# Layer 1's FFN down projection turned over: tokens on the partitions, scaled there, transposed back and added to x

## The chip, the core and the metric

The kernel runs on one core of a Trainium2 chip. The metric is the device time of one execution in microseconds. Engines are named as in the profile: PE is TensorE's matrix multiplication and PEld its weight loads, DVE is VectorE, ACT is ScalarE, POOL is GpSimd, SP is SyncE, which here only issues DMAs.

## The reference, cut to what matters

Two layers of a streaming encoder over 256 tokens of width 2048. Each layer ends with a gated convolutional FFN whose output is normalised and added to x. The change touches the last step of layer 1:

```python
def rms_norm(x, g):
    y = x * lax.rsqrt(jnp.mean(x * x, axis=-1, keepdims=True) + NORM_EPS)
    return y * g

def channel_mixer(h, up, conv_w, conv_b, down):      # h (256, 2048), up (2048, 8192), down (4096, 2048)
    hid = causal_dwconv(h @ up, conv_w, conv_b)
    gate, val = jnp.split(hid, 2, axis=-1)
    return (jax.nn.gelu(gate, approximate=True) * val) @ down

f = channel_mixer(h, ffn_up[layer], ffn_conv_w[layer], ffn_conv_b[layer], ffn_down[layer])
x = x + rms_norm(f, ffn_post_g[layer])               # for layer 1 this is the output
```

## The kernel before

**Layout.** x lies in SBUF as xT, 128 partitions by 16 feature tiles by 256 tokens: features are on the partitions, tokens in the free dimension. The output leaves in the same order, so that the runs of a DMA that writes all tokens of n feature tiles are n KB long on each partition.

**Precision by three products.** Every float32 weight piece is split into a high part wh and a rest wl, both float32r. An activation tile x has a high and a low half too. A product is wh·x.hi + wl·x.hi + wh·x.lo. In the form called WIDE the two halves of x lie side by side and form one moving operand of 512 columns: for each weight tile of 128 x 128 one matmul of 512 columns with wh as the weights (L225) and one of 256 columns with wl (L228). In the narrow form there are three matmuls of 256 columns (function three, L208 to L210). Function tok_chunk, which layer 0 uses for its value projection, does it the other way round: the activation tile is loaded as the weights, and 512 columns of wh or wl are streamed (L300 to L302), with one accumulator bank for each of the two tiles of 128 tokens.

**Pieces.** Weights come in pieces of 2 tiles of 128 rows by 512 columns (512 KB), issued on SP's queue into 4 raw buffers. ACT makes wh (L155), DVE makes wl (L156), each with 5 buffers. Function take hands the next piece to the caller and, before it does so, emits the splits up to 4 pieces ahead and the DMAs behind them. The order of the pieces is a list written out in advance (plan). Function between runs jobs that fell due after a piece; in layer 1's down projection no job is queued. Within an engine the order is the program's, except that an instruction that is ready earlier can be placed ahead of one that is not.

**Layer 1's down projection, norm and last sum.** out_proj makes four chunks of 512 output features, each over 32 tiles of the hidden width, that is 16 pieces. In the first three chunks the form is WIDE, one bank for each tile of 128 features; when a chunk is complete, ACT copies one half of each bank, DVE adds the other (merge), ACT squares the result, DVE sums the squares, and ACT multiplies by the gain (gained). In the fourth chunk two of its four tiles take the narrow form, so that they need no merge. A product with a matrix of ones adds the squares up over the partitions and gives every partition the sum for each token (L749, L757). Then finish takes the root (root, L353 to L359) and goes through the 16 feature tiles in the hand-written order TAIL: DVE and POOL take turns with one or two tiles, multiply by the root (L463), add x (L464) and write out, DVE's parts on SP's queue and POOL's on ACT's (L465).

**SBUF tiles.** The normalised input xg of this FFN lies in the hpool tiles H6, H10, H7 and H8 and is read for the last time by the last up projection chunk. The projected output mg lies in H6 and H10.

Of the kernel before, what the change touches and what calls it, by code (L numbers as in the profile page):

```python
# [9 lines left out]
F32 = mybir.dt.float32  # L10
F32R = mybir.dt.float32r
I32 = mybir.dt.int32
AF = mybir.ActivationFunctionType
# [3 lines left out]
P = 128  # L17
T = 256
D = 2048
# [14 lines left out]
ROOT = 15  # L34
EARLY = 6
SINGLE = 2

TAIL = (("v", 1), ("p", 1), ("v", 2), ("p", 1), ("v", 2), ("p", 1), ("v", 2), ("p", 1), ("v", 2), ("p", 1), ("v", 2))
LRU_EARLY = 4
BEF = 3  # L40


# [17 lines left out]
def trunk(ctx: ExitStack, tc: tile.TileContext, a: dict, out: bass.AP):  # L60
# [10 lines left out]
    def nm(s):  # L71
        cnt[0] += 1
        return f"{s}_{cnt[0]}"
# [4 lines left out]
    def w2(shape):  # L78
        return spool.tile(shape, F32, tag="w2", name=nm("w2"), bufs=7)

    def acc_bank(shape):
        return psum.tile(shape, F32, tag="ps", name=nm("acc"))

    def ms_bank(shape):
        return psum.tile(shape, F32, tag="ps", name=nm("ms"))
# [73 lines left out]
    def behind_pieces(fn):  # L159

        with tc.issue_after(state["act"].ins), tc.issue_after(state["dve"].ins):
            return fn()
# [8 lines left out]
    def take(tag):  # L171
        i = state["take"]
        state["take"] += 1
        ahead(i + PIECES - 1)
        j = jobs[i]
        assert j["tag"] == tag, (j["tag"], tag)
        return j["hi"], j["lo"], j["k0"], j["n"]
# [4 lines left out]
    def later(pieces, fn):  # L182
        state["seq"] += 1
        queue.append((state["count"] + pieces, state["seq"], fn))
# [126 lines left out]
    def big(idx, dt=F32):  # L311
        return [H(i, dt) for i in idx]
# [21 lines left out]
    def at(b):  # L334
        def f(k, n=None):
            t = b[k // 8]
            return t[:, k % 8, :] if n is None else t[:, k % 8:k % 8 + n, :]
        return f
# [6 lines left out]
    def bc(r, n=2):  # L345
        return r[:, None, :].to_broadcast([P, n, T])


    def root(ps, n, tag, with_table=None, with_step=None):

        r = spool.tile([P, T], F32, tag=f"r_{tag}", name=nm("rstd"))
        t = w1()
        i = nc.scalar.activation(r, ps, AF.Abs_reciprocal_sqrt, bias=eps_c[:, 0:1], scale=1.0 / n)  # L353
        early = with_table(r, i) if with_table else None
        nc.vector.scalar_tensor_tensor(t, r, -0.5 / n, r, op0=ALU.mult, op1=ALU.mult)
        nc.vector.scalar_tensor_tensor(t, ps, n * EPS, t, op0=ALU.add, op1=ALU.mult)
        if with_step:
            with_step(t, early)
        nc.vector.scalar_tensor_tensor(r, t, 1.5, r, op0=ALU.add, op1=ALU.mult)  # L359
        return r  # L360
# [90 lines left out]
            else:  # L451
                later(k - EARLY + 1, lambda k=k: step(k, 2))

    def finish(mg, st):
        st["rest"]()
        rs = root(st["ps"], D, "post")
        ft = big((7, 8))
        k = 0
        for e, n in TAIL:
            eng = nc.vector if e == "v" else nc.gpsimd  # L460
            xs = xT[:, k:k + n, :]
            t = ft[k // 8][:, k % 8:k % 8 + n, :]
            eng.tensor_tensor(t, mg(k, n), bc(rs, n), op=ALU.mult)  # L463
            eng.tensor_tensor(xs, xs, t, op=ALU.add)  # L464
            (nc.sync if e == "v" else nc.scalar).dma_start(out[:, k:k + n, :], xs)  # L465
            k += n


    S0, S1 = slice(0, P), slice(P, P + T)
# [298 lines left out]
    def ffn(layer, mg, st, xgi, hi_, mgi):  # L768
# [42 lines left out]
        load_table(last[-1])  # L811
        if layer == 0:
            later(4, lambda: behind_pieces(tables))
        mg2 = at(big(mgi))
        st2 = out_proj(f"d{layer}", layer, hid, 32, "ffn_post_g", mg2, ("mix_pre_g", 1) if layer == 0 else None)
        return mg2, st2
# [268 lines left out]
    mg = at(big((4, 5)))  # L1085
    st = out_proj("cdo", 1, oc + od, 16, "mix_post_g", mg, ("ffn_pre_g", 1), CD_ORDER)
    flush()
    mg, st = ffn(1, mg, st, (6, 10, 7, 8), (9, 11, 0, 1, 2, 3, 4, 5), (6, 10))
    finish(mg, st)


# [48 lines left out]
```

## Time and profile before

| what | value |
|---|---|
| time, median of 3 runs | 1745.57 us (1744.69 to 1745.91) |
| the profiled execution's own time | 1744.74 us |
| its span, from the first to the last instruction | 1743.0 us |
| PE busy | 1721.8 us (99% of the span) |
| PEld busy | 1551.9 us (89%) |
| DVE busy | 1221.3 us (70%) |
| ACT busy | 983.6 us (56%) |
| POOL busy | 37.8 us (2%) |
| DMA traffic | 314.92 MB, 181 GB/s in the mean |

Busy times of PE overlap each other, since matmuls are pipelined: the distance between the starts of two matmuls is what each costs, not its own duration. The chain that ended last is the sequence of instructions that, followed back from the end, each set the start of the next. The granted clock is given as a share of 2.4 GHz.

### The profile page before, as it was taken

The page shows a single profiled execution, that of the slowest core. Times are in us where ns is not written, and L with a number is a line of the kernel's source. Part 1 is how long each engine was busy: PE and PEld are TensorE (multiplying, and loading weights), DVE is VectorE, ACT ScalarE, POOL GpSimd, SP SyncE. Part 2 cuts the span into 40 slices and gives each one's busy share as a digit, 9 for nine tenths or more (in the row PEclk, how much of TensorE's full clock was granted, in tenths as well). Part 3 has the DMA queues.
Part 4 walks back from the last instruction along what each step waited for, and adds up shares of the span by engine and source line. Part 5 has one row for each costly group of instructions (what it writes and reads, how often), then busy time and mean ns, then how long its engine had stood idle before and what let it go on. Part 6 is the DMA issues. An engine that isn't in the chain of part 4 may idle for free.

```text
span 1743.0 us, 27768 instructions
## 1 busy us (share of the span) xinstructions
PE 1721.8 (99%) x10786; PEld 1551.9 (89%) x10786; DVE 1221.3 (70%) x1839; ACT 983.6 (56%) x1511; POOL 37.8 (2%) x117
## 2 busy tenths in 40 slices
PE   9999999999999999999999999999999999999995
PEld 9888888999888888888999999899988888888895
DVE  7675667588777777855468996658877777774544
ACT  6445554566555555654446875656655555554441
POOL 0000000000000000000000010000000000000002
PEclk9999999999999999999999999999999999999998
DMA  8566555655666666565556545555566666656552
GB/s 275 175 208 188 157 154 170 184 161 179 198 189 192 186 190 192 185 195 189 185 159 180 158 146 166 173 183 162 176 205 186 189 193 186 190 192 187 189 182 72
DMA packets 165027, 314.92 MB, mean 181 GB/s; under 512 B 12064, under 2 KB 15264, under 8 KB 164896
## 3 DMA queue, kind: packets, MB, share of 16 engines
q1 hardware_dynamic: 163184, 310.13, 58.0%
q0 software_dynamic: 560, 2.10, 0.4%
q8 instruction: 84, 1.38, 0.3%
q10 hardware_dynamic: 1152, 0.93, 0.2%
q14 instruction: 47, 0.39, 0.1%
HBM read 311.02 MB, written 2.10 MB: 180 GB/s over the span
## 4 chain that ended last, share of the span: by engine, by line
PE 96%; DVE 3%; ACT 1%; issue 0%; DMA 0%; DVEq 0%; ACTq 0%
PE acc L225 47%; PE acc L228 24%; PE acc L208 5%; PE acc L210 5%; PE acc L209 5%; PE ms L209 2%; PE ms L208 2%; PE ms L210 2%; PE acc L300 1%; PE acc L302 1%; PE acc L301 1%; DVE wl L156 1%; PE ms L717 0%; PE ms L497 0%; PE ms L905 0%
## 5 line engine op out<-in xcount | busy, mean ns | idle before, releaser
L156 DVE TENSOR_TENSOR wl<-wr,wh 128x1024 fp32r<-128x1024 f32 (+2 forms) x592 | 714.7, 1211 | 459.3 <-ACT wh L155 457.7
L155 ACT CAST wh<-wr 128x1024 fp32r<-128x1024 f32 (+2 forms) x592 | 611.9, 1037 | 598.4 <-PE acc L225 360.4
L225 PE MATMUL acc<-H,wh 128*128 128x512 f32 x3520 | 912.9, 394 | 0.0
L225 PEld LDWEIGHTS acc<-H,wh 128*128 128x128 f32 x3520 | 621.7, 189 | 100.0
L228 PEld LDWEIGHTS acc<-H,wl 128*128 128x128 f32 x3520 | 502.3, 190 | 49.4
L228 PE MATMUL acc<-H,wl 128*128 128x256 f32 x3520 | 515.4, 282 | 0.0
L208 PE MATMUL acc<-H,wh 128*128 128x256 f32 (+1 forms) x736 | 210.8, 287 | 0.8 <-ACT H L391 0.8
L209 PE MATMUL acc<-H,wl 128*128 128x256 f32 (+1 forms) x736 | 207.7, 282 | 0.0
L210 PE MATMUL acc<-H,wh 128*128 128x256 f32 (+1 forms) x736 | 207.5, 283 | 0.0
L208 PEld LDWEIGHTS acc<-H,wh 128*128 128x128 f32 (+1 forms) x736 | 139.1, 189 | 1.8 <-ACT H L391 1.4
L209 PEld LDWEIGHTS acc<-H,wl 128*128 128x128 f32 (+1 forms) x736 | 139.1, 189 | 0.3
L210 PEld LDWEIGHTS acc<-H,wh 128*128 128x128 f32 (+1 forms) x736 | 139.0, 189 | 0.0
L283 ACT COPY w<-acc 128x256 f32<-128x256 f32 x192 | 70.3, 370 | 64.2 <-PE acc L228 64.2
L208 PE MATMUL ms<-H,wh 128*128 128x256 f32 x256 | 73.0, 285 | 0.0
L209 PE MATMUL ms<-H,wl 128*128 128x256 f32 x256 | 72.3, 283 | 0.0
L210 PE MATMUL ms<-H,wh 128*128 128x256 f32 x256 | 72.3, 283 | 0.0
L787 ACT ACTIVATE w<-w,pk 128x256 f32<-128x256 f32 x128 | 69.4, 593 | 1.7 <-DVE w L781 1.2
L788 DVE SCALAR_TENSOR_TENSOR w<-w,pk,w 128x256 f32<-128x256 f32 x128 | 56.7, 481 | 1.3 <-ACT w L787 1.1
L789 DVE SCALAR_TENSOR_TENSOR w<-w,pk,w 128x256 f32<-128x256 f32 x128 | 56.2, 480 | 0.0
L284 DVE TENSOR_TENSOR w<-acc,w 128x256 f32<-128x256 f32 x120 | 49.8, 420 | 2.8 <-ACT w L283 1.1
L208 PEld LDWEIGHTS ms<-H,wh 128*128 128x128 f32 x256 | 49.1, 192 | 0.1
L209 PEld LDWEIGHTS ms<-H,wl 128*128 128x128 f32 x256 | 49.1, 192 | 0.1
(225 smaller groups left out, 1101.7 us busy)
## 6 DMA issues: line engine op xcount, KB each, us to landing
wr<-in_ffn_up SPq DMA_DIRECT2D x256, 512.0 KB, 4.5
wr<-in_ffn_down SPq DMA_DIRECT2D x128, 512.0 KB, 3.9
wr<-in_ab_w_in SPq DMA_DIRECT2D x78, 512.0 KB, 3.6
wr<-in_cd_w_in SPq DMA_DIRECT2D x40, 512.0 KB, 4.4
wr<-in_ab_w_out SPq DMA_DIRECT2D x32, 512.0 KB, 4.4
wr<-in_cd_w_out SPq DMA_DIRECT2D x32, 512.0 KB, 4.2
wr<-in_w_q_up SPq DMA_DIRECT2D x8, 384.0 KB, 3.9
wr<-in_cd_w_in SPq DMA_DIRECT2D x8, 320.0 KB, 3.0
```

What stands on the lines that cost most here:

```text
L155: state["act"] = nc.scalar.copy(hi, j["raw"])
L156: state["dve"] = nc.vector.tensor_tensor(lo, j["raw"], hi.bitcast(F32), op=ALU.subtract)
L208: nc.tensor.matmul(ps, wh, x.hi(k), start=start, stop=False, skip_group_check=True)
L209: nc.tensor.matmul(ps, wl, x.hi(k), start=False, stop=False, skip_group_check=True)
L210: return nc.tensor.matmul(ps, wh, x.lo(k), start=False, stop=stop, skip_group_check=True)
L225: mm = nc.tensor.matmul(banks[b], hi[:, kk, c], x.both(korder[i] if korder else i), start=i == 0, stop=False, skip_group_check=True)
L228: mm = nc.tensor.matmul(banks[b][:, 0, :], lo[:, kk, c], x.hi(korder[i] if korder else i), start=False, stop=i == ks - 1, skip_group_check ...
L283: nc.scalar.copy(t, bank[:, 1, :])
L284: nc.vector.tensor_tensor(dst, bank[:, 0, :], t, op=ALU.add)
L787: nc.scalar.activation(t[:, j, :], u[:, j, 2:], AF.Identity, scale=cw[2], bias=col("ffn_conv_b", layer, i))
L788: nc.vector.scalar_tensor_tensor(t[:, j, :], u[:, j, 1:1 + T], cw[1], t[:, j, :], op0=ALU.mult, op1=ALU.add)
L789: nc.vector.scalar_tensor_tensor(t[:, j, :], u[:, j, 0:T], cw[0], t[:, j, :], op0=ALU.mult, op1=ALU.add)
```

## The change

Layer 1's last projection no longer goes through out_proj and finish. Function last_sum, called at the end of ffn for layer 1, does this instead:

- A row of the 2048 gains is gathered by a DMA on POOL's queue from pk (where they lie 128 to a column) to partition 0 of gb, which is H7. Seven more DMAs on the same queue double it: 1 partition to 2, to 4, up to 128. Each needs the one before.
- Chunks 0 to 2 go through tok_chunk. After each, for both token tiles, take_out lets ACT square the bank with the sum along the row collected in ss, and DVE multiply the bank by the gains into u (H6 for token tile 0, H10 for tile 1). Sums are thus scalars per partition, so that no product with ones is needed. The sums of three chunks are added up and prepared for the root (pre_b, pre_n).
- Chunk 3 goes on for 14 pieces with both token tiles in turn. The last two pieces (AHEAD = 4 tiles of the hidden width) are taken together: all 12 matmuls of token tile 0 come first, then 9 of token tile 1, and its last 3 stand in the program behind the first 8 transposes of token tile 0.
- The root of a token tile is one ACT instruction and three DVE instructions of one column (last_root). Four parts of 512 features are scaled by it, on DVE and ACT in turn (scaled). Function back turns a part over with four transposes on PE into one bank, DVE adds the bank to xT, and SP's queue writes out 4 feature tiles by 128 tokens, 256 KB in runs of 512 bytes.
- The table TAIL and function finish are gone, and POOL has no arithmetic left at the end.

```diff
--- before.py
+++ after.py
@@ -34,9 +34,9 @@
 ROOT = 15
 EARLY = 6
 SINGLE = 2
-
-TAIL = (("v", 1), ("p", 1), ("v", 2), ("p", 1), ("v", 2), ("p", 1), ("v", 2), ("p", 1), ("v", 2), ("p", 1), ("v", 2))
 LRU_EARLY = 4
+
+AHEAD = 4
 BEF = 3
 
 
@@ -451,19 +451,103 @@
             else:
                 later(k - EARLY + 1, lambda k=k: step(k, 2))
 
-    def finish(mg, st):
-        st["rest"]()
-        rs = root(st["ps"], D, "post")
-        ft = big((7, 8))
-        k = 0
-        for e, n in TAIL:
-            eng = nc.vector if e == "v" else nc.gpsimd
-            xs = xT[:, k:k + n, :]
-            t = ft[k // 8][:, k % 8:k % 8 + n, :]
-            eng.tensor_tensor(t, mg(k, n), bc(rs, n), op=ALU.mult)
-            eng.tensor_tensor(xs, xs, t, op=ALU.add)
-            (nc.sync if e == "v" else nc.scalar).dma_start(out[:, k:k + n, :], xs)
-            k += n
+    def last_sum(pref, layer, o, ks, gname, u, gb):
+
+
+        u = [t.rearrange("p k t -> p (k t)") for t in u]
+        gb = gb.rearrange("p k t -> p (k t)")
+
+        c0 = _COL[gname][0] + 16 * layer
+        with nc.allow_non_contiguous_dma(reason="a row of gains"):
+            nc.gpsimd.dma_start(gb[0:1, :], a["pk"][:, c0:c0 + KD].rearrange("p k -> k p"))
+        n = 1
+        while n < P:
+            nc.gpsimd.dma_start(gb[n:2 * n, :], gb[0:n, :])
+            n *= 2
+        ss = spool.tile([P, 2, 4], F32, tag="sm", name="ss", bufs=4)
+        pre_b = spool.tile([P, 2], F32, tag="rcol", name=nm("pre"), bufs=2)
+        pre_n = spool.tile([P, 2], F32, tag="rcol", name=nm("pre"), bufs=2)
+        rs = spool.tile([P, 2], F32, tag="rcs", name="rs")
+        tn = spool.tile([P, 2], F32, tag="lz", name="tn")
+
+        def part(c):
+            return slice(512 * c, 512 * c + 512)
+
+        def take_out(c, b, bank):
+            nc.scalar.activation(w2([P, 512]), bank, AF.Square, accum_out=ss[:, b, c:c + 1])
+            nc.vector.tensor_tensor(u[b][:, part(c)], bank, gb[:, part(c)], op=ALU.mult)
+
+        for c in range(3):
+            for b, bank in enumerate(tok_chunk(f"{pref}{c}", o, ks, 512)):
+                take_out(c, b, bank)
+        for b in range(2):
+            nc.vector.tensor_tensor(tn[:, b:b + 1], ss[:, b, 0:1], ss[:, b, 1:2], op=ALU.add)
+            nc.vector.tensor_tensor(tn[:, b:b + 1], tn[:, b:b + 1], ss[:, b, 2:3], op=ALU.add)
+        nc.vector.tensor_scalar(pre_b, tn, 1.0 / D, EPS, op0=ALU.mult, op1=ALU.add)
+        nc.vector.tensor_scalar(pre_n, tn, D * EPS, None, op0=ALU.add)
+
+        banks = [acc_bank([P, 512]) for _ in range(2)]
+
+        def products(b, tiles):
+            for hi, lo, kk, k in tiles:
+                xh, xl = o.hi(k)[:, b * P:(b + 1) * P], o.lo(k)[:, b * P:(b + 1) * P]
+                nc.tensor.matmul(banks[b], xh, hi[:, kk, :], start=k == 0, stop=False)
+                nc.tensor.matmul(banks[b], xh, lo[:, kk, :], start=False, stop=False)
+                mm = nc.tensor.matmul(banks[b], xl, hi[:, kk, :], start=False, stop=k == ks - 1)
+            return mm
+
+        def last_root(b):
+            r, t, s = rs[:, b:b + 1], tn[:, b:b + 1], ss[:, b, 3:4]
+            nc.scalar.activation(r, s, AF.Abs_reciprocal_sqrt, bias=pre_b[:, b:b + 1], scale=1.0 / D)
+            nc.vector.scalar_tensor_tensor(t, r, -0.5 / D, r, op0=ALU.mult, op1=ALU.mult)
+            nc.vector.scalar_tensor_tensor(t, s, pre_n[:, b:b + 1], t, op0=ALU.add, op1=ALU.mult)
+            nc.vector.scalar_tensor_tensor(r, t, 1.5, r, op0=ALU.add, op1=ALU.mult)
+
+        def scaled(b, c):
+            v = u[b][:, part(c)]
+            if c % 2:
+                nc.scalar.activation(v, v, AF.Copy, scale=rs[:, b:b + 1])
+            else:
+                nc.vector.tensor_scalar(v, v, rs[:, b:b + 1], None, op0=ALU.mult)
+
+        def back(b, c):
+            pt = ms_bank([P, 4, P])
+            for j in range(4):
+                nc.tensor.transpose(pt[:, j, :], u[b][:, 512 * c + P * j:512 * c + P * j + P], ident)
+            xs = xT[:, 4 * c:4 * c + 4, b * P:(b + 1) * P]
+            nc.vector.tensor_tensor(xs, xs, pt, op=ALU.add)
+            nc.sync.dma_start(out[:, 4 * c:4 * c + 4, b * P:(b + 1) * P], xs)
+
+        done = 0
+        while done < ks - AHEAD:
+            hi, lo, k0, n = take(f"{pref}3")
+            for kk in range(n):
+                for b in range(2):
+                    mm = products(b, [(hi, lo, kk, k0 + kk)])
+            done += n
+            between(mm)
+        tiles = []
+        while done < ks:
+            hi, lo, k0, n = take(f"{pref}3")
+            tiles += [(hi, lo, kk, k0 + kk) for kk in range(n)]
+            done += n
+        products(0, tiles)
+        take_out(3, 0, banks[0])
+        last_root(0)
+        products(1, tiles[:-1])
+        for c in range(4):
+            scaled(0, c)
+        back(0, 0)
+        back(0, 1)
+        products(1, tiles[-1:])
+        take_out(3, 1, banks[1])
+        back(0, 2)
+        back(0, 3)
+        last_root(1)
+        for c in range(4):
+            scaled(1, c)
+        for c in range(4):
+            back(1, c)
 
 
     S0, S1 = slice(0, P), slice(P, P + T)
@@ -811,6 +895,8 @@
         load_table(last[-1])
         if layer == 0:
             later(4, lambda: behind_pieces(tables))
+        if layer == 1:
+            return last_sum("d1", 1, hid, 32, "ffn_post_g", big(mgi), H(7))
         mg2 = at(big(mgi))
         st2 = out_proj(f"d{layer}", layer, hid, 32, "ffn_post_g", mg2, ("mix_pre_g", 1) if layer == 0 else None)
         return mg2, st2
@@ -1085,8 +1171,7 @@
     mg = at(big((4, 5)))
     st = out_proj("cdo", 1, oc + od, 16, "mix_post_g", mg, ("ffn_pre_g", 1), CD_ORDER)
     flush()
-    mg, st = ffn(1, mg, st, (6, 10, 7, 8), (9, 11, 0, 1, 2, 3, 4, 5), (6, 10))
-    finish(mg, st)
+    ffn(1, mg, st, (6, 10, 7, 8), (9, 11, 0, 1, 2, 3, 4, 5), (6, 10))
 
 
 # ---- launch: one core ----
```

## Rows read from the trace of the kernel before

**Rows 1.** Busy time by stage, whole windows: window, length, engines, clock, DMA, GB/s
```profile
1541.60:1675.60 134.00, 134.00 (x770) 117.83 (x769) 72.70 (x83) 64.38 (x87) 0.00 (x0) 1.00 0.60 189
1675.60:1724.40 48.80, 48.80 (x341) 45.60 (x341) 20.66 (x25) 19.33 (x31) 0.00 (x0) 1.00 0.34 108
1724.40:1743.00 18.60, 1.13 (x5) 0.33 (x3) 13.33 (x15) 1.91 (x5) 10.69 (x10) 0.59 0.32 113
```

**Rows 2.** Chain that ended last, in the tail: start, length, engine and line
```profile
1724.28 0.14 PE acc L210
...
1727.81 1.55 DVE H L463 x2
```

**Rows 3.** Timeline of PE, chunks 0 and 3 of the down projection: start, busy time
```profile
1541.61 0.63 PE L225 MATMUL acc<-H,wh 128*128 128x512 f32 x2
...
1675.67 0.63 PE L225 MATMUL acc<-H,wh 128*128 128x512 f32 x2
...
1703.96 1.09 PE L225 MATMUL acc<-H,wh 128*128 128x512 f32 x4
```

**Rows 4.** Timeline of PE in layer 0's value projection, the token form
```profile
57.29 0.40 PE L300 MATMUL acc<-wh,H 128*128 128x512 f32 x1
...
59.82 0.39 PE L302 MATMUL acc<-wh,H 128*128 128x512 f32 x1
...
89.19 0.39 PE L301 MATMUL acc<-wl,H 128*128 128x512 f32 x1
...
108.23 0.39 PE L301 MATMUL acc<-wl,H 128*128 128x512 f32 x1
```

**Rows 5.** DMA issues by line: KB each, us from issue to landing
```profile
out_x<-xT SPq DMA_DIRECT2D x5, 256.0 KB, 2.1
...
H<-in_lru_wa POOLq DMA_DIRECT2D x1, 512.0 KB, 6.2
...
pk<-in_pk ACTq DMA_DIRECT2D x1, 8.0 KB, 3.0
```

**Rows 6.** Groups of instructions by line, shapes apart: busy us, mean ns
```profile
L883 POOL DMA_DIRECT2D H<-in_lru_wa x1 | 0.9, 899 | 189.1 <-PE acc L210 189.1
L481 ACT ACTIVATION_READ_ACCUMULATOR w<-w,sm 128x1 f32 x32 | 6.0, 187 | 0.0
L399 ACT ACTIVATE w<-acc 128x256 f32<-128x256 f32 x8 | 3.1, 384 | 6.4 <-PE acc L210 6.4
L659 ACT ACTIVATE H<-acc,rcol 128x512 f32<-128x512 f32 x4 | 2.8, 690 | 2.3 <-PE acc L302 2.3
L783 DVE TENSOR_TENSOR w<-ms,rstd 128x512 f32<-128x512 f32 x4 | 2.7, 684 | 0.0
L103 ACT ACTIVATE eps_c<-eps_c 128x1 f32<-128x1 f32 x6 | 1.2, 203 | 0.1
L637 DVE TENSOR_SCALAR score<-w,wT 128x256 f32<-128x256 f32 x1 | 0.3, 344 | 0.0
L637 DVE TENSOR_SCALAR score<-w,wT 128x128 f32<-128x128 f32 x1 | 0.3, 280 | 0.0
L839 DVE TENSOR_SCALAR lz<-pk 128x8 f32<-128x8 f32 x1 | 0.2, 163 | 0.0
```

**Rows 7.** Timeline of PE, three transposes of 128 x 128 in a row
```profile
176.57 0.49 PE L490 MATMUL ms<-ident,w 128*128 128x128 f32 x3
```

**Rows 8.** Timeline of DVE in the tail, its last adds
```profile
1731.28 2.34 DVE L463 TENSOR_TENSOR H<-H,rstd 128x512 f32<-128x512 f32 x2
...
1738.06 1.80 DVE L464 TENSOR_TENSOR xT<-xT,H 128x512 f32<-128x512 f32 x2
```

**Rows 9.** DMA queues from 1725 us on: packets, MB, share of 16 engines' 18.1 us
```profile
q1 hardware_dynamic: 864, 1.44, 21.5%
q10 hardware_dynamic: 720, 0.66, 10.9%
```

**Rows 10.** Busy time by window in the tail, with the granted clock
```profile
1728.00:1730.00 2.00, 0.00 (x0) 0.00 (x0) 2.00 (x3) 0.00 (x0) 2.00 (x3) 0.50 0.00 0
```

## The prediction

> **What bounds the kernel now.** I read the busy time by stage first, cut at the start of layer 1's down projection and at its last matmul. From 1541.6 to 1724.4 us PE is busy all the time at the full granted clock, DVE and ACT about half of it, and the DMA engines a third to 60% [rows 1]. So 182.8 us go at PE's pace, and a change there counts only if it alters the number or the spacing of matmuls. The last 18.6 us are another stage: PE has 1.1 us of work, DVE 13.3, POOL 10.7. The chain of waits, read next, shows it in order: a last matmul from 1724.28 to 1724.42, then square and root, and from 1727.81 on DVE's multiplications and adds only [rows 2]. DVE's adds of 128x512 take far longer there than its usual 0.684 us: the four multiplications and adds in a row from 1731.28 to 1735.88 need about 1.15 each, with POOL at work on the same kind beside it [rows 6, 8]. The last add ends at 1738.06 + 1.80 = 1739.86; the span ends at 1743.0, so 3.14 us are the write-out and what closes the program [rows 8, 1]. Two stages, two separate terms.
>
> **The matmuls' spacing.** Before, piece 1 of chunk 0 starts at 1541.61 and piece 1 of chunk 3 at 1675.67, with 48 pieces between: 2.793 us a piece [rows 3]. In chunk 3, with two tiles in the narrow form, ten pieces take 1703.96 - 1675.67 = 28.29, 2.829 each [rows 3]. A piece in token form is 12 matmuls of 512 columns: as many columns as before (3072 per tile of the hidden width), in 12 instructions where there were 16 or 20. What one costs there is in layer 0's value projection: undisturbed, 84 matmuls from 89.19 to 108.23, 0.2267 each; at its start, behind another form, 11 from 57.29 to 59.82, 0.230 each [rows 4]. So a piece costs 2.72 (at worst 2.76). There the activation is the loaded operand too, and the loads of it are hidden behind 512 columns, so I carry it over; I take the undisturbed value, because no queued job breaks into these chunks. By 62 pieces (all but the last two) the time before would be 48 x 2.793 + 14 x 2.829 = 173.7; after, 62 x 2.72 = 168.7 (at worst 171.1). **Term one: -5.0 us** (bounds -2.6 and, if the trace's spacing does not carry over, 0). The last two pieces then start at t0 = 1541.61 + 168.7 = 1710.3.
>
> **Work beside PE.** Squares and multiplications at the chunk ends (two of each, 0.7 to 0.8 us each) are fewer than the copies, merges, squares, sums and gains that they replace; DVE and ACT have more than 40% spare [rows 1] and up to four split pieces lie ready, so they cost nothing. Without that cover, a delay of DVE would stop PE after four pieces, 10.9 us.
>
> **The row of gains.** It can start when H7 is free, at 1541.6, and is needed at the first take_out, 16 x 2.72 = 43.5 us later. No row shows such a gather. Nearest are three: pk's 8 KB in 3.0 us, lru_wa on POOL's queue in 6.2 us for 1024 runs of 512 bytes, and 2.1 for an output of 256 KB [rows 5]; POOL spends 0.9 on issuing one [rows 6]. Gather: from 0.9 + 3.0 to 0.9 + 2 x 6.2 (2048 runs), 3.9 to 13.3. Each doubling: 0.9 + 2.1 to 0.9 + 6.2, 3.0 to 7.1, seven times. Sum 25 to 63 us. Six doublings are small, nearest to pk's 3.9, the last carries 512 KB, 7.1; with the gather at its upper end this is 13.3 + 6 x 3.9 + 7.1 = 44 us. That is level with 43.5. But DVE waits behind prepared pieces: a multiplication that is stuck holds up the splits of L156 queued behind it, and PE feels this only when the four pieces are used up, less one split, some 8 us later. The limit is 51.5 us, so I put this at nothing; the upper end would stall PE by 63 - 51.5 = 11.5 us.
>
> The Trainium skill's page "DMA: Bandwidth & Descriptors" (section Rules for kernel authors) speaks against this gather: a last dim that isn't contiguous becomes one descriptor per element, so 2048 of 4 bytes. By its section Anatomy of one DMA (about 2.0 us fixed for each DMA from GpSimd, the bytes at 436 GB/s) the eight DMAs, about 1 MB, would need an estimated 18.4 us beside what the descriptors cost. The sum would be the same by either. No run here shows the gather.
>
> **The tail, from t0.** Token tile 0's 12 matmuls start at 0; the last one begins at 11 x 0.2267 = 2.5 and ends 0.39 later, at 2.9. ACT's square of 512 from PSUM: 0.384 for 256 [rows 6], about 0.6 for 512, plus 0.187 to read the sum, to 3.75; the root on one column 0.2 [rows 6], to 4.0. DVE's three small steps at 0.163 [rows 6] end at 4.6. Scaling on DVE: 0.280 for 128 columns and 0.344 for 256 [rows 6] give 0.47 for 512 by the same slope; on ACT 0.69 [rows 6]. PE is through with token tile 1's 9 matmuls at 21 x 0.2267 = 4.75 and can turn over the first part at 5.2, three transposes in a row take 0.49 [rows 7], so four at most 0.65. Whether PE's last three matmuls come before or after the first transposes, they end by 6.9.
>
> From 5.85 on DVE decides. Adds from PSUM take 0.684 [rows 6]: two adds to 7.2, the multiplication of token tile 1 to 7.9, two adds to 9.25, the root to 9.75 (its square has long been done on ACT), two scalings to 10.7, a first add at 10.95, the fourth done at 13.7. Some 0.03 us between DVE instructions, 14 of them, make it **14.2**. Before, it was 1739.86 - (1541.61 + 173.7) = 24.5 behind the same place in the pieces.
>
> Behind it, the write-out. It was 3.14 us with runs of 1 and 2 KB. From the queues: 864 packets of 1.67 KB on average took 0.215 x 16 x 18.1 = 62 us of engine time, 72 ns each; 720 of 0.92 KB took 44 ns [rows 9]. That line gives some 29 ns at 0.5 KB; 512 such runs over 16 engines are 0.93 us for 256 KB, against 0.7 between adds. Three times 0.2 late: 0.6 us. Bounds: 0 if transfers are absorbed, 1.5 if a 0.5 KB run costs 44 ns like the larger ones. End: 1710.3 + 14.2 + 3.14 + 0.6 = **1728.2**, against 1743.0: **-14.8 us** in all, so -9.8 for the tail. One cost I leave at zero: PE waits some 3 us for token tile 1's scaling, and in the old tail, in a window in which PE had nothing, the clock stood at 0.50 [rows 10]; four transposes at half clock are 0.9, which would add 0.2 to each of four adds, 0.8 us.
>
> The profiled execution took 1744.74, 0.83 below the median of 1745.57; taken off the median, this is **1730.8 us**.
>
> **Rivals.**
> 1. *PE's spacing does not improve.* The ready DMA and split work could hold it at 2.79, since the fast stretch is only 19 us of another layer. Against it: that stretch ran beside the same splits. Term one falls away: 1735.8. Chance 0.1.
> 2. *The gains come late.* By the rows the chain is 25 to 63 us with 51.5 allowed; for it speaks that my middle (44) is near. PE stalls by up to 11.5 us: 1731 to 1742, about 1737. Chance 0.1.
> 3. *Slower: the gather runs on one DMA engine.* It ends in a single partition, and its 2048 elements might all go through one queue. lru_wa's 1024 runs on 16 engines are 64 each in 6.2 us, 97 ns a run; 2048 in one queue would be 199 us, and with doublings of 30.5 the stall is 199 + 30.5 - 51.5 = 178 us: about 1909. It decides from a gather of 51.5 + 14.8 - 30.5 = 35.8 us upward, 17.5 ns an element: that eats the whole gain. Against it: a load of 8 KB took 3.0 us, though in other runs [rows 5]. Chance 0.06. Beside this stands the page's rule "Use all 16 engines" (same section): the engines are chosen by the access patterns' slowest dim, here 16 tiles at the source; by that the gather is spread.
>
> **How the numbers follow.** The forecast has 0.74. Its own range is 1728 (write-out free, DVE at 13.7) to 1735 (spacing 0.230: +2.4; runs of 0.5 KB: +0.9; half clock: +0.8). The whole range goes to 1738, which takes in rival 1 and half of rival 2, and to 1727.5 below. A difference under 0.2%, 3.5 us, can't be told from none here: all of the forecast and rival 1 and most of rival 2 lie below 1742. Faster 0.91, same 0.02, slower 0.07.
>
> **What would show it.** L300-like matmuls in layer 1 at 0.227 spacing, and a first matmul of the last two pieces near 1710; POOL's eight DMAs over before 1585, DVE's first gain multiplication not waiting for a DMA; the last matmul of a product near 1717; DVE without gaps of more than 0.3 us from its first scaling to its last add near 1724.5, with adds near 0.69 since POOL is silent; the last landing some 3 to 4 us later. I am wrong if PE idles in chunk 1, if PE's pieces take 2.79, or if the write-out queues up by microseconds.

## The result, and the profile after

The changed kernel takes **1734.03 us** (median of 6 runs, 1733.01 to 1734.96); the kernel before, on the same chip, 1745.74 (6 runs, 1744.69 to 1746.76). The ratio is 0.9933 [0.9924, 0.9943], a difference of 11.7 us. The profiled execution of after took 1733.38 with a span of 1731.6, against 1744.74 and 1743.0: its spans differ by 11.4 us, and that is the sum to be explained.

The page's line of busy times, of the changed kernel:

```profile
PE 1719.7 (99%) x10492; PEld 1538.4 (89%) x10492; DVE 1210.5 (70%) x1829; ACT 976.2 (56%) x1486; POOL 31.8 (2%) x115
```

PE is busy for all but 11.9 us of the span. To see where, the windows of layer 1's down projection, cut by the new code (columns as in [rows 1]):

```profile
1545.00:1713.70 168.70, 168.70 (x747) 139.68 (x746) 84.78 (x90) 72.03 (x83) 3.72 (x8) 1.00 0.61 186
1713.70:1720.40 6.70, 6.65 (x35) 5.34 (x34) 2.63 (x8) 2.32 (x5) 0.00 (x0) 1.00 0.00 0
1720.40:1731.60 11.20, 3.29 (x25) 2.65 (x23) 6.28 (x14) 2.32 (x5) 0.00 (x0) 0.72 0.66 187
```

These are the pieces up to the last two, then the matmuls of these two, then the tail. The first answers to the two first windows of [rows 1]: PE without a gap at full clock. The last answers to their third: 11.2 us where there were 18.6, with POOL silent.

Where does the projection begin? The timeline of PE, changed kernel:

```profile
1542.22 0.63 PE L225 MATMUL acc<-H,wh 128*128 128x512 f32 x2
...
1544.77 0.40 PE L228 MATMUL acc<-H,wl 128*128 128x256 f32 x2
1545.01 0.40 PE L300 MATMUL acc<-wh,H 128*128 128x512 f32 x1
...
1713.67 0.39 PE L494 MATMUL acc<-wh,H 128*128 128x512 f32 x1
```

The first new matmul (L300) is at 1545.01. In the 2.79 us ahead of it stands a piece of the old form, in which L225 and L228 take turns in twos. [rows 3] have the same pattern at 1541.61, and the prediction took it for the projection's first piece. It is the *last piece of the chunk before* (a chunk's last piece does its products bank by bank). So the projection of the kernel before starts at 1541.61 + 2.79 = 1544.40, which the timeline of that kernel shows too. Its last two pieces start at 1718.13:

```profile
1544.40 1.09 PE L225 MATMUL acc<-H,wh 128*128 128x512 f32 x4
...
1718.13 1.09 PE L225 MATMUL acc<-H,wh 128*128 128x512 f32 x4
```

From here on **S** is the first matmul of layer 1's down projection: 1544.40 before, 1545.01 after. S differs from profile to profile (1544.4 to 1546.4 in the runs below), and between before and after the difference is there from the start: PE's first matmul of L270 begins at 5.54 before and at 6.13 in after. Executions of one kernel differ as much (spans of 1731.2 to 1733.2 for after). So profiles are compared by their distance from S.

The chain of waits at the end, changed kernel:

```profile
1716.59 0.70 ACT w L477 x2
1717.31 0.69 DVE H L478
...
1718.56 0.50 DVE H L511
1719.10 0.67 PE ms L516 x4
1719.79 1.88 DVE xT L518 x3
1721.67 0.60 DVE H L478
1722.28 0.59 DVE xT L518
...
1723.43 0.50 DVE H L511
1723.97 0.67 PE ms L516 x4
1724.66 1.88 DVE xT L518 x3
1726.55 0.60 DVEq L1221
```

It reads as the prediction's tail did: square (L477), gain (L478), scaling (L511), transposes (L516), adds (L518), once for each token tile, with tile 1's gain between tile 0's adds. What is new is that the gain follows the square of the same bank instead of running beside it. PE's wait for tile 1's scaling, put at some 3 us, is 2.67 (up to 1723.97). The timeline gives the same with the idle times:

```profile
1717.31 0.69 DVE L478 TENSOR_TENSOR H<-acc,H 128x512 f32<-128x512 f32 x1 [9.29 <-ACT w L477]
...
1720.46 0.60 ACT L477 ACTIVATE w<-acc 128x512 f32<-128x512 f32 x1 [0.57 <-PE acc L496]
...
1723.97 2.39 PE L516 MATMUL ms<-ident,H 128*128 128x128 f32 x16 [2.67 <-DVE H L511]
1724.66 2.48 DVE L518 TENSOR_TENSOR xT<-xT,ms 128x512 f32<-128x512 f32 x4 [0.35 <-PE ms L516]
```

The last add ends at 1724.66 + 2.48 = 1727.14, and 4.46 us later the span ends. The three terms, then, with t0 as the first matmul of the last two pieces:

| | before | after | change | forecast |
|---|---|---|---|---|
| S to t0 | 173.73 | 168.66 | -5.1 | -5.0 |
| t0 to the last add's end | 21.73 | 13.47 | -8.3 | -10.4 |
| last add's end to the span's end | 3.14 | 4.46 | +1.3 | +0.6 |
| S itself | 1544.40 | 1545.01 | +0.6 | 0 |
| span | 1743.0 | 1731.6 | **-11.4** | -14.8 |

(t0 is 1718.13 before and 1713.67 after, by the rows above.)

### The profile page after: what moved, and what is told of

It is laid out like the page before. It is cut to its first block, busy times and chain, and to the rows that moved or that the text cites. A ratio compares the mean times of both kernels' runs of the same rounds, so it can differ in the third digit from the quotient of the medians.

```text
span 1731.6 us, 27137 instructions
## 1 busy us (share of the span) xinstructions
PE 1719.7 (99%) x10492; PEld 1538.4 (89%) x10492; DVE 1210.5 (70%) x1829; ACT 976.2 (56%) x1486; POOL 31.8 (2%) x115
## 4 chain that ended last, share of the span: by engine, by line
PE 96%; DVE 3%; ACT 1%; issue 0%; DMA 0%; DVEq 0%; ACTq 0%
PE acc L225 41%; PE acc L228 21%; PE acc L208 4%; PE acc L210 4%; PE acc L209 4%; PE acc L300 3%; PE acc L301 3%; PE acc L302 3%; PE ms L209 2%; PE ms L210 2%; PE ms L208 2%; PE acc L495 1%; PE acc L496 1%; PE acc L494 1%; DVE wl L156 1%; PE ms L801 0%
## 5 line engine op out<-in xcount | busy, mean ns | idle before, releaser
L225 PE MATMUL acc<-H,wh 128*128 128x512 f32 x3072 | 797.8, 394 | 0.0
L225 PEld LDWEIGHTS acc<-H,wh 128*128 128x128 f32 x3072 | 542.3, 189 | 87.0
L228 PEld LDWEIGHTS acc<-H,wl 128*128 128x128 f32 x3072 | 438.9, 190 | 43.5
L228 PE MATMUL acc<-H,wl 128*128 128x256 f32 x3072 | 450.4, 282 | 0.0
L208 PE MATMUL acc<-H,wh 128*128 128x256 f32 (+2 forms) x672 | 192.5, 287 | 0.8 <-ACT H L391 0.8
L209 PE MATMUL acc<-H,wl 128*128 128x256 f32 (+2 forms) x672 | 189.7, 282 | 0.0
L210 PE MATMUL acc<-H,wh 128*128 128x256 f32 (+2 forms) x672 | 189.4, 283 | 0.0
L208 PEld LDWEIGHTS acc<-H,wh 128*128 128x128 f32 (+2 forms) x672 | 126.9, 189 | 1.7 <-ACT H L391 1.4
L209 PEld LDWEIGHTS acc<-H,wl 128*128 128x128 f32 (+2 forms) x672 | 127.0, 189 | 0.3
L210 PEld LDWEIGHTS acc<-H,wh 128*128 128x128 f32 (+2 forms) x672 | 126.8, 189 | 0.0
L300 PE MATMUL acc<-wh,H 128*128 128x512 f32 x256 | 100.5, 393 | 0.0
L301 PE MATMUL acc<-wl,H 128*128 128x512 f32 x256 | 99.7, 389 | 0.0
L302 PE MATMUL acc<-wh,H 128*128 128x512 f32 x256 | 99.6, 389 | 0.0
L300 PEld LDWEIGHTS acc<-wh,H 128*128 128x128 f32 x256 | 48.0, 188 | 11.5 <-issue 1.3
```

The costliest lines, as they stand in the source:

```text
L208: nc.tensor.matmul(ps, wh, x.hi(k), start=start, stop=False, skip_group_check=True)
L209: nc.tensor.matmul(ps, wl, x.hi(k), start=False, stop=False, skip_group_check=True)
L210: return nc.tensor.matmul(ps, wh, x.lo(k), start=False, stop=stop, skip_group_check=True)
L225: mm = nc.tensor.matmul(banks[b], hi[:, kk, c], x.both(korder[i] if korder else i), start=i == 0, stop=False, skip_group_check=True)
L228: mm = nc.tensor.matmul(banks[b][:, 0, :], lo[:, kk, c], x.hi(korder[i] if korder else i), start=False, stop=i == ks - 1, skip_group_check ...
L300: nc.tensor.matmul(banks[b], xhk, hi[:, kk, :], start=done + kk == 0, stop=False)
```

## Experiments

All runs in one table; each was timed against the kernel before, whose medians were 1745.2 to 1745.3 in these runs. "Square" is the start of ACT's square of the last bank, "add" the end of the last add. The distances from S come from one profile each; after, e2_late2 and e5_runs, which go through the same steps in the tail, agree within 0.1.

| run | median us | ratio | span's end from S | square, add from S |
|---|---|---|---|---|
| before | 1745.74 | 1 | 198.6 | -, 195.5 |
| after | 1734.03 | 0.9933 [0.9924, 0.9943] | 186.6 | 175.5, 182.1 |
| e1_wide | 1737.50 | 0.9953 [0.9939, 0.9968] | 190.1 | 179.0, 185.8 |
| e2_late2 | 1733.83 | 0.9940 [0.9923, 0.9956] | 186.5 | |
| e2_late4 | 1737.13 | 0.9956 [0.9940, 0.9972] | 186.8 | |
| e4_tail_dve | 1743.23 | 0.9988 [0.9978, 0.9997] | 196.5 | -, 193.1 |
| e9_no_lead | 1735.43 | 0.9944 [0.9927, 0.9960] | 187.9 | 174.6, 183.4 |
| e3_ahead8 | 1734.39 | 0.9934 [0.9919, 0.9948] | 186.2 | 175.2, 181.8 |
| e3b_turned | 1732.59 | 0.9926 [0.9911, 0.9941] | 186.2 | 176.1, 181.8 |
| e5_runs | 1733.45 | 0.9933 [0.9917, 0.9950] | 186.5 | |
| e7_runs2 | 1733.30 | 0.9931 [0.9916, 0.9946] | 185.7 | -, 182.1 |
| e6_short | 1732.92 | 0.9928 [0.9913, 0.9943] | 186.0 | 176.1, 181.5 |
| e8_short2 | 1731.75 | 0.9923 [0.9910, 0.9935] | 185.0 | 176.1, 181.5 |

**Is the first term the spacing of matmuls?** e1_wide gives chunks 0 to 2 back their old form, and keeps the new tail. The columns in its banks are not those that the later steps need, so its output is not the layer's; only its time is read.

```diff
-            for b, bank in enumerate(tok_chunk(f"{pref}{c}", o, ks, 512)):
-                take_out(c, b, bank)
+            wide = chunk(f"{pref}{c}", o, ks, F4, layout=WIDE)
+            for b in range(2):
+                take_out(c, b, wide[b].rearrange("p a t -> p (a t)"))
```

> The changed kernel, but chunks 0 to 2 use the WIDE form again (its columns are not the ones that the later steps need: the output is not the reference's). Evacuation, gains and tail stay as they are. My theory, that the spacing of the matmuls is the whole of term one: a piece goes back from 2.72 to 2.793 us, the 48 pieces take 3.5 us longer, and the span grows by 3.5. Rival, that the chunks end earlier for another reason (lighter evacuation, fewer waits at the chunk ends): the span grows by under 1 us. Token form after a WIDE chunk should show the same 0.2267 spacing in chunk 3.

The timeline of e1_wide has PE's first matmul of the projection at 1544.45 and ACT's square of tile 0 in its last chunk here:

```profile
1719.53 0.60 ACT L477 ACTIVATE w<-acc 128x512 f32<-128x512 f32 x1 [9.82 <-PE acc L497]
```

That is S + 175.1; in after it is 1716.59 - 1545.01 = 171.6. So 3.5 us lie in 48 pieces, 0.073 a piece, as 2.793 - 2.72 says. From there on both take the same time: the span ends 15.1 us behind tile 0's square in this run, 15.0 in after. The whole run is 3.5 us longer from S and by median. Term one is the matmuls' spacing, and 3.5 of its 5.1 us are shown by this run; the other 1.6 are chunk 3, where only the traces of before and after speak.

**Do the gains come late, and what if they did?** In after POOL starts the gather at 1539.89. The DMA issues of after from 1535 to 1600 us (KB each, us from issue to landing):

```profile
H<-H POOLq DMA_DIRECT2D x1, 512.0 KB, 6.2
...
H<-in_pk POOLq DMA_DIRECT2D x1, 8.0 KB, 13.0
H<-H POOLq DMA_DIRECT2D x1, 8.0 KB, 4.0
```

and, of POOL's timeline, the gather, the first doubling and the last:

```profile
1539.89 1.05 POOL L462 DMA_DIRECT2D H<-in_pk  x1 [30.47 <-PE acc L228]
1553.17 0.52 POOL L465 DMA_DIRECT2D H<-H  x1 [12.23 <-DMA H<-in_pk]
...
1581.49 0.52 POOL L465 DMA_DIRECT2D H<-H  x1 [5.89 <-DMA H<-H]
```

The chain ends at 1581.49 + 6.2 = 1587.7, 47.8 us after it began. The first multiplication with the gains is at 1588.26, behind a split and with no idle time ahead of it:

```profile
1587.12 1.23 DVE L156 TENSOR_TENSOR wl<-wr,wh 128x1024 fp32r<-128x1024 f32 x1 [1.50 <-ACT wh L155]
1588.26 0.68 DVE L478 TENSOR_TENSOR H<-acc,H 128x512 f32<-128x512 f32 x1
```

So they came in time by some 0.6 us. To see what lies behind that edge, two runs make the chain longer by copying the last half again, twice (the diff) and four times:

```diff
+        for _ in range(2):
+            nc.gpsimd.dma_start(gb[P // 2:P, :], gb[0:P // 2, :])
```

> The changed kernel with two more copies of the upper 512 KB behind the seven doublings of the gains, 6.7 us each. The gains then land some 56 us after the first matmul of the projection instead of 42.7, and DVE's first gain multiplication, due at 43.3, waits 12.8. My theory, four split pieces less one split (8 us) hidden: PE stalls once in chunk 1, by about 4.6 us, and the span grows by as much. Rival one, no cover: 12.8 us longer. Rival two, all of it hidden by lighter chunks: under 0.5 us.

> The changed kernel with four more copies of 512 KB behind the doublings. With two, the gains landed 54.5 us after the first matmul of the projection, DVE stood still for 8.8 us, and PE did not wait. Theory: the cover is five prepared pieces, 13.6 us, less what DVE must do first when the gains come (two multiplications and a split, 2.5 us), so that the limit is about 55 us. The gains should land at 67 to 69; PE then stalls 12 to 14 us in chunk 1 and the span grows by as much. Rival: there is more slack (raw pieces, lighter chunks): under 6 us.

DVE's timeline, first of e2_late2, then of e2_late4:

```profile
1599.01 1.29 DVE L480 TENSOR_TENSOR H<-acc,H 128x512 f32<-128x512 f32 x2 [7.85 <-DMA H<-H]
```

```profile
1599.20 1.22 DVE L156 TENSOR_TENSOR wl<-wr,wh 128x1024 fp32r<-128x1024 f32 x1 [1.50 <-ACT wh L155]
1609.34 1.29 DVE L480 TENSOR_TENSOR H<-acc,H 128x512 f32<-128x512 f32 x2 [8.92 <-DMA H<-H]
```

In e2_late2 DVE stands for 7.85 us (the expectation of e2_late4 has 8.8) until the DMA lands, at S + 54.5, and PE waits for nothing: the prepared pieces cover it, and the stall of 4.6 us that the first theory had did not come. In e2_late4 the multiplication is at S + 63, 8.6 us later, but DVE's wait is only 8.92 us, 1.1 longer. The number of splits between S and the multiplication explains this: 16 in after, 17 in e2_late2, 20 in e2_late4. With a longer chain the multiplication stands behind more splits in DVE's order. PE pays once, in its weight loads:

```profile
1611.82 0.19 PEld L301 LDWEIGHTS acc<-wl,H 128*128 128x128 f32 x1 [0.34 <-DVE wl L156]
```

So the slack is larger than the 51.5 us of the prediction: the old theory of what a late chain costs fell in both profiles, 0 and 0.3 us where it had 4.6 and 12 to 14. What stays open: the five executions of e2_late4 run from 1734.75 (the profiled one) to 1742.46, with a median 3.1 above after's, and of the four of e2_late2 one took 1737.12, where the longest of after took 1734.96. A later landing would explain the longer ones, since at 8.92 us of DVE's wait PE waits too, but none of them was profiled.

**What did POOL do in the old tail?** e4_tail_dve is the kernel *before*, with all of its tail on DVE:

```diff
-TAIL = (("v", 1), ("p", 1), ("v", 2), ("p", 1), ("v", 2), ("p", 1), ("v", 2), ("p", 1), ("v", 2), ("p", 1), ("v", 2))
+TAIL = (("v", 2),) * 8
```

> The kernel before with all eight parts of its last sum on DVE (two feature tiles each, written out on SP's queue), none on POOL. Theory, POOL beside DVE slowed DVE's instructions from 0.69 to about 1.15 us, so its help was worth nothing: 16 instructions of 0.69 to 0.72 us end 11.0 to 11.5 us after the root against 12.05, and the span is 0.5 to 1 us shorter. Rival, POOL's five tiles of sixteen are real help: without it DVE needs 5/11 more, the span grows by 3 to 5 us.

Its DVE timeline, the first and the last of eight rows of two instructions:

```profile
1727.99 1.29 DVE L463 TENSOR_TENSOR H<-H,rstd 128x512 f32<-128x512 f32 x2
...
1736.43 1.28 DVE L464 TENSOR_TENSOR xT<-xT,H 128x512 f32<-128x512 f32 x2
```

Sixteen instructions of 512 columns start 0.60 us apart and are done in 9.72 us (1727.99 to 1737.71). Before, DVE had twelve, two of them half as wide, and needed 12.05 (1727.81 to 1739.86), about 1.15 for each wide one [rows 8], while POOL did the rest. The kernel gets faster by 2.1 us from S, and by 2.0 in the median: taking 5 of the 16 blocks off DVE had cost more than it saved, and by more than was expected. So 2.1 of the 6.9 us that the change wins in its tail were to be had by POOL's silence alone. On this the Trainium skill's page "SBUF — State Buffer" (section Who interferes with whom) says that a DVE instruction with two inputs in SBUF contends with a GpSimd instruction that reads SBUF, and that the pair of ports that they share is an exclusive lock. The trace agrees that the two contend; that DVE's spacing grew from 0.60 to 1.15, beside POOL instructions of 1.07 on average [rows 1], fits turns taken, but the records don't show which of the two was held.

**What is the head start of token tile 0 worth?** e9_no_lead lets the tiles take turns to the end (AHEAD = 0, the products behind the loop left out); e3_ahead8 doubles the head start; e3b_turned doubles it and also moves tile 0's transposes between tile 1's matmuls.

```diff
-AHEAD = 4
+AHEAD = 0
...
-        products(0, tiles)
...
-        products(1, tiles[:-1])
...
-        products(1, tiles[-1:])
```

That is e9_no_lead; e3_ahead8 has only the first line, with 8. e3b_turned has 8 too, and this order:

```diff
-        products(1, tiles[:-1])
+        products(1, tiles[:5])
...
         back(0, 0)
         back(0, 1)
-        products(1, tiles[-1:])
-        take_out(3, 1, banks[1])
+        products(1, tiles[5:6])
         back(0, 2)
         back(0, 3)
+        products(1, tiles[6:])
+        take_out(3, 1, banks[1])
```

> The changed kernel without the lead of token tile 0: in all 16 pieces of chunk 3 both tiles take turns, and tile 0's chain begins 0.7 us before the last matmul's end. The last matmul starts 1.0 us earlier than in the changed kernel (no transposes and no wait of PE before it). Theory, without the lead DVE must do both tiles' work after the matmuls: two gain multiplications, two roots, four scalings, eight adds, 9 to 9.6 us behind tile 0's square: the last add ends some 184.2 after the projection's first matmul in place of 182.1, and the span 1.5 to 2.5 us later than 186.6. Rival, the lead is worth nothing since tile 1's own chain sets the end and PE's wait is saved: no longer than 186.6, up to 1 us less.

> The changed kernel with token tile 0 four pieces ahead in place of two (AHEAD 8). Its square, root, scaling, transposes and adds start 2.7 us earlier; the last matmul stays where it is. Theory one, DVE is the bound from the first scaling to the end, so that all it does earlier is gained: 2 to 2.7 us shorter. Theory two, token tile 1 has a chain of its own (square, gain multiplication, root, scaling, transposes, four adds, write-out) that starts only with its last matmul, and DVE's work for tile 0 costs it only one add and a wait, about 0.9 us: 0.5 to 1 us shorter.

> The changed kernel with token tile 0 four pieces ahead, and now its transposes stand among token tile 1's matmuls: 15 matmuls, 8 transposes, 3 matmuls, 8 transposes, 6 matmuls. Tile 0's adds are over when tile 1's last matmul ends. Counted from the first matmul of the projection, the span of the changed kernel ends at 186.6. Theory two (tile 1's chain from its last matmul on sets the end): the gain multiplication follows the square at once and no add of tile 0 stands between, 0.9 to 1.1 us earlier, 185.5 to 185.7. Theory one (DVE is full, what it does earlier is gained): 2 to 2.7 us earlier, 183.9 to 184.6.

Without a lead the last add ends 1.3 us later and the span too (187.9 against 186.6). That is less than was expected: tile 1's last product comes earlier, since no transposes stand between (its square starts at S + 174.6, not 175.5). What is left of the 6.9 us, some 3.5 if this 1.3 and POOL's 2.1 add up, no run isolates; it is read from the two timelines only. The row of the last adds in e9_no_lead:

```profile
1726.62 2.48 DVE L518 TENSOR_TENSOR xT<-xT,ms 128x512 f32<-128x512 f32 x4 [0.36 <-PE ms L516]
```

e3_ahead8 tested nothing: tile 0 was scaled earlier, but its transposes stood in PE's program behind 21 of tile 1's matmuls, and DVE waited for them.

```profile
1720.47 1.28 DVE L518 TENSOR_TENSOR xT<-xT,ms 128x512 f32<-128x512 f32 x2 [2.35 <-PE ms L516]
```

e3b_turned mended that. From tile 1's square to the end of the last add it takes 5.68 us where after takes 6.68, the 1.0 that was expected, since DVE has only tile 1 left. Its square, however, starts 0.63 later from S, because all 16 transposes of tile 0 now stand ahead of PE's last matmul. Net 0.4.

**What does the write-out cost?** Each of the eight output DMAs carries 256 KB in runs of 0.5 KB. e5_runs reorders the output tensor so that its runs in memory are 2 KB (the host only puts the elements back in order); e7_runs2 also has DVE write its sums into a tile where they lie 2 KB in a row.

```diff
-            nc.sync.dma_start(out[:, 4 * c:4 * c + 4, b * P:(b + 1) * P], xs)
+            flat = out.rearrange("p k t -> p (k t)")[:, 512 * (4 * b + c):512 * (4 * b + c) + 512]
+            nc.sync.dma_start(flat.rearrange("p (j t) -> p j t", j=4), xs)
```

```diff
-            nc.vector.tensor_tensor(xs, xs, pt, op=ALU.add)
+            y = u[b][:, part(c)]
+            nc.vector.tensor_tensor(y.rearrange("p (j t) -> p j t", j=4), xs, pt, op=ALU.add)
...
+            nc.sync.dma_start(flat, y)
```

> The changed kernel with an output tensor in the order in which the parts are made (token tile, part, feature tile, token), so that each write-out of 256 KB has runs of 2 KB in place of 512 bytes; the host only reorders. Theory, 512-byte runs hold the DMA engines at 285 GB/s and the last megabyte leaves slower (3.7 us) than DVE's four adds make it (2.5 us): with 2 KB runs at 385 GB/s it takes 2.7 us, and from the last add's end to the span's end it is 3.3 to 3.6 us in place of 4.46; the span ends some 1 us earlier, at 185.6 from the first matmul of the projection. Rival, the last 256 KB and its latency alone set the end: under 0.3 us.

> The changed kernel with the reordered output tensor, and DVE's last adds written into u (2 KB in a row on each partition) in place of xT, so that a write-out has runs of 2 KB on both sides. With the reordering of the output alone the DMA engines still moved 4224 packets of about 0.5 KB at 285 GB/s, since the rows in xT were still 512 bytes long. Theory, the shorter of the two sides sets the packets and they set the rate: now some 1150 packets, 380 GB/s, and 3.3 to 3.6 us from the last add's end to the span's end in place of 4.46; the span ends 1 us earlier, 185.4 to 185.7 from the projection's first matmul. Rival, the last transfer's latency sets the end: under 0.3 us.

The DMA view of the last 12 us: GB/s in 40 slices of 0.3 us, the packets by size, and the issues. First after, then e7_runs2:

```profile
GB/s 0 0 0 0 0 0 237 251 321 275 280 302 284 259 321 278 290 295 103 0 0 0 176 258 319 275 266 317 272 276 307 282 288 295 164 0 0 0 0 0
DMA packets 4224, 2.10 MB, mean 175 GB/s; under 512 B 128, under 2 KB 4224, under 8 KB 4224
...
out_x<-xT SPq DMA_DIRECT2D x8, 256.0 KB, 2.7
```

```profile
GB/s 0 0 0 0 0 0 0 0 7 369 403 362 403 355 416 300 7 369 396 109 0 0 0 0 0 348 355 410 341 417 348 423 355 410 89 0 0 0 0 0
DMA packets 1152, 2.10 MB, mean 175 GB/s; under 512 B 128, under 2 KB 128, under 8 KB 1152
...
out_x<-H SPq DMA_DIRECT2D x8, 256.0 KB, 2.1
```

With runs of 0.5 KB the engines move about 285 GB/s, 0.92 us for 256 KB, while DVE hands over 256 KB every 0.60: the four DMAs of a tile queue up, and the span ends 4.46 us behind the last add (the DMA engines are idle for its last 1.5). With 2 KB it is about 385 GB/s, 0.68 us, and the span ends 3.54 behind. That is the 0.92 that was expected of e7_runs2. e5_runs did nothing, and its DMA view says why: the packets are still as small, since the source rows in SBUF are 0.5 KB:

```profile
DMA packets 4224, 2.10 MB, mean 175 GB/s; under 512 B 128, under 2 KB 4224, under 8 KB 4224
```

**All of it together.** e6_short is e3b_turned with e5's output, and with the last chunk's gain and scaling in one instruction, which takes the gain off the way between tile 1's square and root (the scalings of parts 1 and 2 are then ACT's). e8_short2 is the same with e7's write-out.

```diff
+            if c == 3:
+                nc.vector.scalar_tensor_tensor(v, banks[b], rs[:, b:b + 1], gb[:, part(3)], op0=ALU.mult, op1=ALU.mult)
```

> The two before it together, and the last part of each token tile goes from PSUM through one DVE instruction that multiplies by root and gain at once, so that no gain multiplication stands before the root; parts 1 and 2 are scaled on ACT. Tile 1's chain: square and its sum 0.8, root 0.9, DVE's scaling 0.45, fused part 0.7, four adds 2.5, write-out 3.4. Expected if tile 1's own chain sets the end: last add 5.6 to 5.9 us after the last matmul (6.7 in the changed kernel), span end 183.9 to 184.5 from the projection's first matmul, 2.1 to 2.7 us earlier. If DVE's sum of work set it, about 4 us earlier.

> All three together: token tile 0 four pieces ahead with its transposes among tile 1's matmuls, the fused last part, and write-outs with runs of 2 KB on both sides. Without the last of these the span ended 186.0 after the projection's first matmul, the last add 5.42 after the first square of tile 1's last part began and the write-out 4.5 after that. Expected: last add unchanged, write-out 3.3 to 3.6, span end 184.8 to 185.2, some 1.5 to 1.8 us less than the changed kernel. Rival, no gain of the write-out: 186.0.

e6_short ended 1.5 to 2.1 us later than expected: the square starts as late as in e3b_turned, and the write-out stayed at 4.5 because of the 0.5 KB rows in SBUF. e8_short2 came out as expected, 185.0 from S. Its last rows in the timeline:

```profile
1720.67 0.60 ACT L477 ACTIVATE w<-acc 128x512 f32<-128x512 f32 x1 [4.19 <-PE acc L497]
...
1723.59 2.48 DVE L522 TENSOR_TENSOR H<-xT,ms 128x512 f32<-128x512 f32 x4
```

It is the fastest of all, 1731.75 us and 1.6 us below after by the distance from S; the two ratios' intervals overlap, so of this only the profile is sure.

## Why the prediction was right, and where it was wrong

The sign, the mechanism and the range held (1734.03 lies in 1727.5 to 1738.0). The point was 3.2 us too low, and one step accounts for most of that.

- **The step that failed: "t0 = 1541.61 + 168.7 = 1710.3", and with it "24.5 behind the same place in the pieces".** The piece at 1541.61 is the last of the chunk before, so everything that was counted from it stood 2.79 us too early. The number of pieces and their spacing do not depend on it, so term one is not touched but for the place of one piece (the ten pieces put at 2.829 hold one of the old form; chunk 3's own take 2.833). But the tail of before was measured from the wrong place: it is 21.7 us to the last add, and 24.9 to the span's end where the prediction had 27.7. The gain of the tail was overstated by that 2.8. The row itself could have told: its pattern, two and two, is not the one at 1544.40, where L225 comes four in a row. Another 0.6 us is S, later in the new profile from its first matmuls on; that is no work of the change. 14.8 - 2.8 - 0.6 = 11.4, the difference of the spans.
- **Term one** was right: 168.66 us from S to t0, forecast 168.7. The undisturbed spacing of [rows 4] carried over, and rival 1 fell (e1_wide).
- **The tail from t0** was right as a sum, 17.93 against 14.2 + 3.14 + 0.6 = 17.94, by luck: two errors cancel. To the last add it took 13.47, not 14.2: DVE's instructions start 0.60 apart although each shows 0.68, and the sum went by 0.68 and added gaps. The write-out took 4.46, not 3.74: 0.92 us for 256 KB was the right price, but an add hands over the next 256 KB after 0.60, not 0.7, and three times 0.32 makes 0.96 of the 1.3 by which it grew. By the rates of e7_runs2 the last transfer itself is an estimated 0.24 longer (0.92 against 0.68); the small rest was not looked into.
- **Two bounds** do not follow from the prediction's own terms. At 44 ns a run 256 KB take 1.41 us, and three times 1.41 - 0.7 is 2.1, not 1.5. A free write-out and DVE at 13.7 give 1729.7, not 1728. The measured terms lie inside either way.
- **DVE's order:** the gain of a bank does not run beside ACT's square of it but after it (1717.31, 9.3 us idle until ACT), and three adds of tile 0, not two, go ahead of tile 1's gain. This was left out of the sum, and it sits inside the 13.47.
- **The half clock** was left at zero, and in the profile after it cost nothing. While PE waits for tile 1's scaling the granted clock is still 1.00; it falls to 0.50 only when the transposes are under way, and the adds do not feel it:

```profile
1722.00:1724.00 2.00, 0.03 (x1) 0.03 (x1) 1.89 (x7) 0.57 (x1) 0.00 (x0) 1.00 1.04 291
1724.00:1726.00 2.00, 2.00 (x16) 1.96 (x16) 1.65 (x4) 0.76 (x2) 0.00 (x0) 0.84 0.57 160
1726.00:1728.00 2.00, 0.36 (x2) 0.00 (x0) 1.14 (x2) 0.00 (x0) 0.00 (x0) 0.50 0.86 242
```

  The 16 transposes take 2.39 there and 1.97 in e8_short2 and e9_no_lead, where the granted clock is 1.00 throughout; the four adds behind them take 2.48 in all three. Four of them in 2.39 / 4 = 0.60 us are still level with DVE's 0.60 an add. It was close: in e5_runs and e2_late4 the 16 transposes take 2.59 and 2.61, and the adds wait for them and take 2.62 and 2.63. In e2_late2 and e7_runs2, with the same wait of PE, they take 1.97, so the moment of the fall is not fixed by this wait alone.
- **The gains** came without a wait, as forecast, but through a sum whose parts were off. The gather took 13.0 us, at the upper bound; the doublings were 3.5 to 6.5 us each; the chain was 47.8, not 44, and began at 1539.89. Against that stands the estimate from the Trainium skill's page "DMA: Bandwidth & Descriptors" (section Anatomy of one DMA), 18.4 us beside the price of its descriptors: the measurement decides, and the chain was two and a half times that. The descriptors of the gather are not the reason alone, since the seven doublings took 34.5 of the 47.8 us. Rival 2 did not occur, and e2_late2 shows by its profile and its median (1733.83) that 11.8 us more would not have made it one; rival 3 (one DMA engine) would have been a gather of 199 us, and fell.

Of the signs that the prediction named, the spacing of 0.227, no wait of the first gain and adds near 0.69 held. The eight DMAs were not over before 1585 but at 1587.7. DVE has two gaps above 0.3 us, both of 0.35, for the first transposes of each tile (1719.79 and 1724.66). The places (t0 near 1710, last matmul near 1717, last add near 1724.5) are 2.6 to 3.4 us later, for the reason above and by the 0.6 of S.

## What to carry to other kernels

Before a distance in the trace is taken as a term, pin its first end: find the instruction that can belong only to the new stage, and compare the pattern of the pieces beside it, since the same lines of code serve the end of one chunk and the start of the next. When a second engine helps with the same kind of work, look at the helped engine's spacing with and without it; here the help was worth less than nothing. And when the last stage ends in a stream of stores, compare the time that a store takes with the time between two of them, and look at the runs on both sides of the transfer.

## What the runs showed of the hardware

- DVE's 128x512 instructions start 0.60 us apart in a row while each is shown with 0.68 (16 in 9.72 us, e4_tail_dve). Beside POOL's work of the same kind it was about 1.15 for each wide one.
- The size of a store's packets went by the shorter run of its two sides: 4224 packets with 0.5 KB in SBUF, whether memory had 0.5 KB (after) or 2 KB (e5_runs), and 1152 only when both had 2 KB (e7_runs2); about 285 against 385 GB/s.
- A gather of 2048 elements of 4 bytes took 13.0 us, with the weights' stream beside it at 207 GB/s on average (1535 to 1600 us). Copies within SBUF of 8 KB and 512 KB, issued by POOL in the same stretch, took 4.0 and 6.2: 64 times the bytes in 1.6 times the time.
